# Two blocks of a hybrid model: half of the expert output kept in PSUM over all pairs, squares summed on GpSimd, attention order on TensorE written by hand

## The chip, the cores and the metric

One core of one Trainium2 chip runs the whole program in one launch. The metric is the device time of an execution in microseconds (us); 1607.19 us is the median of three runs of the kernel before (1606.79 to 1609.19). TensorE is called PE here, VectorE DVE, ScalarE ACT, GpSimd POOL and SyncE SP, as in the profile.

## The reference

The sequence has 512 tokens of width 1024, all in float32. The first block is a pre-norm block with six modulation vectors; its mixer is causal attention of 8 heads (with a forget gate) beside a pooling mixer, and its second half a gated feed-forward net with a short convolution:

```python
h = _rmsnorm(x, norm1_g[l]) * (1.0 + sc1) + sh1
z = h @ w_in[l]
attn = _fox_attention(q, k, v, log_f)
pool = _multiscale_pool(u, pool_w[l], pool_scale[l])
x = x + g1 * (concatenate([attn, pool]) @ w_out[l])
h = _rmsnorm(x, norm2_g[l]) * (1.0 + sc2) + sh2
x = x + g2 * _conv_ffn(h, ffn_up[l], ffn_conv_w[l], ffn_conv_b[l], ffn_down[l])
return _rmsnorm(x, final_g)
```

The second block has neighbourhood attention (8 heads, with an RMS norm of its output) beside a gated delta net, and a mixture of 64 experts of width 256, two to a token:

```python
x = x + concatenate([attn, dn], axis=-1) @ w_out
x = x + hierarchical_moe(rms_norm(x, ln2_g), ...)
hid = jax.nn.silu(xb @ w_gate[e]) * (xb @ w_up[e])
return hid @ w_down[e]
```

## The kernel before, in words

Activations lie transposed in SBUF, 128 features by 512 tokens a tile (xT, eight of them). A float32 product is made of three products of split operands, hi x hi, lo x hi and hi x lo (L171 to L173, the rows named pj); ACT makes the hi part (whi, hh: L164, L188) and DVE the lo part (wlo, hl: L165, L190 to L194). PSUM has eight banks, handed out by tags: mm, pa and pb two each, pc and gv one each (the function ps).

Most of the program is ordered by the framework's scheduler, which interleaves the instructions of independent parts on each engine. Two kinds of place are written in order by hand on PE: those inside a manual_schedule block, and before the change only the expert stage is one.

**Sums of squares.** An RMS norm over features is a sum over partitions. ColSums.add (L290) squares a tile on ACT (sq, L292) and multiplies it on PE by a 128x32 tile of ones (cs, L294), into one of four quarters of a bank. done (L297) copies the bank to SBUF on ACT (part, L299) and makes four small products with a weight column (cst, L302); rsqrt4 and row_bcast (rb, L321) follow. It is used for norm1 (col_sums), for norm2 (n2, eight squares, between the tiles of w_out), for the final norm and the second block's first norm together (csA and csB, eight squares each, between the tiles of the feed-forward's last third), and for the norm of the neighbourhood attention's output (cs, four squares).

**First attention.** head_pair(m) (L436) treats two heads. For each of four query tiles i it makes the logits of both heads (pS, L453, 64 rows of the array each), the softmax on DVE and ACT (L459 to L468), and the transposes of the probabilities (pT, L473) with their copies to SBUF (PT, L478 and L480). Then eight products with the values (po, L484). The scheduler sets projections of the next parts between these.

**Neighbourhood attention.** na_pairs has 32 units of a head and a tile: logits (nS, L772), softmax, and out (L783): two transposes (nT, L790), a copy on ACT, two products (npo, L794).

**Experts.** moe_round walks over 32 pairs of experts, expert pr_ with pr_ + 32. On PE, in this written order, are gate_up of a pair (pgu, L1568, 32 products), down of the pair before (pd, L1597, two halves n of eight products; the halves are scaled and split by ACT and DVE into og, hi and lo: L188 and L192), turn (phT, L1582, with the copies hT and OT), and combine of the pair before (L1604): for both halves n and four token tiles t, two products put the pair's rows back to their tokens (pcmb, L1610 and L1611) in one of four banks, and DVE adds the bank to the result xn (L1613). SP issues the weights' loads ahead of use (wgu at L1267, wd at L1277), each as soon as PE frees a buffer.

## Time and profile before

| | |
|---|---|
| median of three runs | 1607.19 us (1606.79 to 1609.19) |
| the profiled execution | 1610.31 us, span 1608.5 us |
| PE busy | 1519.7 us (94%), mean granted clock 0.973 |
| DVE / ACT / POOL busy | 893.3 / 507.8 / 208.7 us |
| chain that ended last | PE 78%, DVE 8%, DMA 5% of the span |
| DMA | 327.24 MB, 203 GB/s over the span |

The profile shows one execution. Its times are in microseconds from the first instruction. The granted clock is TensorE's clock as a share of full speed. A PE product's busy time overlaps that of the next one, since products are pipelined; the step from start to start is what one costs in a row of products. A float32 product that isn't split shows as two passes, so x2 in a row of the timeline is one product of cs, pS or po. What stands in brackets behind a row is the idle time ahead of it and what ended it.

### The profile page before, as it was taken

The page shows a single profiled execution, that of the slowest core. Times are in us where ns is not written, and L with a number is a line of the kernel's source. Part 1 is how long each engine was busy: PE and PEld are TensorE (multiplying, and loading weights), DVE is VectorE, ACT ScalarE, POOL GpSimd, SP SyncE. Part 2 cuts the span into 40 slices and gives each one's busy share as a digit, 9 for nine tenths or more (in the row PEclk, how much of TensorE's full clock was granted, in tenths as well). Part 3 has the DMA queues.
Part 4 walks back from the last instruction along what each step waited for, and adds up shares of the span by engine and source line. Part 5 has one row for each costly group of instructions (what it writes and reads, how often), then busy time and mean ns, then how long its engine had stood idle before and what let it go on. Part 6 is the DMA issues. An engine that isn't in the chain of part 4 may idle for free.

```text
span 1608.5 us, 20691 instructions
## 1 busy us (share of the span) xinstructions
PE 1519.7 (94%) x7541; PEld 1001.7 (62%) x7541; DVE 893.3 (56%) x1797; ACT 507.8 (32%) x937; POOL 208.7 (13%) x290
## 2 busy tenths in 40 slices
PE   6989999999999999998789999977999999999997
PEld 2756676788888886777667888864434434434443
DVE  3768666663564455256797666444445445445445
ACT  3553434442342344354334535410111111111111
POOL 0233000000000000223552330002100000000000
PEclk8979999999999999998989999988999999999999
DMA  8663132333223222354332133558899999999983
GB/s 310 224 208 113 66 132 77 119 99 99 92 98 99 92 81 77 101 165 112 89 104 75 36 88 95 213 237 314 320 406 419 418 415 419 417 413 417 409 364 107
DMA packets 81743, 327.24 MB, mean 203 GB/s; under 512 B 17624, under 2 KB 21336, under 8 KB 57312
## 3 DMA queue, kind: packets, MB, share of 16 engines
q1 hardware_dynamic: 80192, 320.58, 53.9%
q0 software_dynamic: 1440, 5.24, 0.9%
q8 instruction: 62, 1.02, 0.2%
q14 instruction: 49, 0.40, 0.1%
HBM read 317.32 MB, written 8.47 MB: 203 GB/s over the span
## 4 chain that ended last, share of the span: by engine, by line
PE 78%; DVE 8%; DMA 5%; issue 3%; POOL 3%; ACT 2%; SPq 0%; DVEq 0%; POOLq 0%; ACTq 0%
PE pgu L1568 13%; PE pj L171 10%; PE pj L172 10%; PE pj L173 10%; PE pd L1597 7%; PE pcmb L1610 5%; PE pcmb L1611 4%; DMA graw<-in_modw_dram 2%; PE cs L294 2%; PE pS L453 1%; DMA xg<-xs,tok_of 1%; DVE wlo L165 1%; DVE cv L828 1%; PE po L484 1%; PE npo L794 1%
## 5 line engine op out<-in xcount | busy, mean ns | idle before, releaser
L171 PE MATMUL pj<-hh,whi 128*128 128x512 f32 x640 | 258.5, 405 | 17.5 <-ACT cn L822 8.8
L173 PE MATMUL pj<-hh,wlo 128*128 128x512 f32 x640 | 256.2, 401 | 2.4 <-DVE wlo L165 2.4
L172 PE MATMUL pj<-hl,whi 128*128 128x512 f32 x640 | 256.5, 401 | 0.6 <-DVE hl L194 0.6
L1568 PE MATMUL pgu<-wgu,xw 128*64 128x512 f32 x1024 | 226.8, 595 | 0.0
L165 DVE TENSOR_TENSOR wlo<-wraw,whi 128x1024 fp32r<-128x1024 f32 (+4 forms) x126 | 153.1, 1217 | 67.3 <-ACT whi L164 64.1
L164 ACT ACTIVATE whi<-wraw 128x1024 fp32r<-128x1024 f32 (+4 forms) x126 | 129.2, 1028 | 150.5 <-PE pj L172 119.2
L1568 PEld LDWEIGHTS pgu<-wgu,xw 128*64 128x64 f32 x1024 | 70.7, 137 | 139.0 <-issue 138.9
L1613 DVE TENSOR_TENSOR xn<-xn,pcmb 128x512 f32<-128x512 f32 x256 | 155.7, 682 | 0.9 <-PE pcmb L1611 0.9
L171 PEld LDWEIGHTS pj<-hh,whi 128*128 128x128 f32 x640 | 122.7, 192 | 52.5 <-ACT cn L822 11.7
L173 PEld LDWEIGHTS pj<-hh,wlo 128*128 128x128 f32 x640 | 122.8, 192 | 34.3 <-issue 6.9
L172 PEld LDWEIGHTS pj<-hl,whi 128*128 128x128 f32 x640 | 122.8, 192 | 29.6 <-issue 4.4
L1572 ACT ACTIVATE sg<-pgu,agt 128x256 f32<-128x256 f32 x32 | 15.2, 476 | 335.3 <-PE pgu L1568 335.3
L1610 PE MATMUL pcmb<-og,OT 128*128 128x512 f32 x256 | 115.1, 450 | 1.4
L1597 PE MATMUL pd<-wd,hT 128*64 128x512 f32 x512 | 116.3, 596 | 0.0
L1574 DVE SCALAR_TENSOR_TENSOR hid<-pgu,agt,sg 128x256 f32<-128x256 f32 x32 | 15.5, 484 | 174.9 <-ACT sg L1572 174.9
L1611 PE MATMUL pcmb<-og,OT 128*128 128x512 f32 x256 | 101.7, 397 | 0.0
L192 DVE SCALAR_TENSOR_TENSOR og<-pd,agt,og 128x512 fp32r<-128x512 f32 x64 | 48.0, 751 | 77.3 <-ACT og L188 77.3
L1559 POOL COPY xw<-xgT 128x512 f32 x60 | 35.3, 617 | 409.6 <-PE pgu L1568 390.9
L1597 PEld LDWEIGHTS pd<-wd,hT 128*64 128x64 f32 x512 | 36.9, 138 | 73.3 <-issue 73.3
L1610 PEld LDWEIGHTS pcmb<-og,OT 128*128 128x128 f32 x256 | 48.0, 187 | 46.2 <-DVE xn L1613 27.0
L188 ACT ACTIVATE og<-pd,agt 128x512 fp32r<-128x512 f32 x64 | 44.1, 688 | 89.8 <-PE pd L1597 89.8
L172 PE MATMUL pj<-al,whi 128*128 128x512 f32 x176 | 69.8, 397 | 0.0
(430 smaller groups left out, 2499.0 us busy)
## 6 DMA issues: line engine op xcount, KB each, us to landing
wgu<-in_egu_dram SPq DMA_DIRECT2D x128, 1024.0 KB
wd<-in_ed_dram SPq DMA_DIRECT2D x62, 1024.0 KB
graw<-in_modw_dram SPq DMA_DIRECT2D x48, 512.0 KB
wraw<-in_wup_dram SPq DMA_DIRECT2D x42, 512.0 KB
wraw<-in_win_dram SPq DMA_DIRECT2D x38, 512.0 KB
wraw<-in_wdn_dram SPq DMA_DIRECT2D x20, 512.0 KB
wraw<-in_wout_dram SPq DMA_DIRECT2D x16, 512.0 KB
E<-gscr SPq DMA_DIRECT2D x16, 256.0 KB
```

The lines of the kernel that those rows point to most:

```text
L164: nc.scalar.activation(hi, raw, AF.Copy)
L165: nc.vector.tensor_tensor(lo, raw, hi.bitcast(F32), op=ALU.subtract)
L171: nc.tensor.matmul(p, whi, hh, start=first, stop=False)
L172: nc.tensor.matmul(p, whi, hl, start=False, stop=False)
L173: nc.tensor.matmul(p, wlo, hh, start=False, stop=last)
L188: nc.scalar.activation(hi, src, AF.Identity, scale=scale, bias=0.0 if bias is None else bias)
L192: nc.vector.scalar_tensor_tensor(lo, src, scale, hi.bitcast(F32), op0=ALU.mult, op1=ALU.subtract)
L1568: nc.tensor.matmul(gu[64 * i:64 * i + 64, :], xw[:, j, 64 * i:64 * i + 64], wts.gu[e][j], start=(j == 0), stop=(j == 7))
L1597: nc.tensor.matmul(pd[64 * i:64 * i + 64, :], hT[:, j, 64 * i:64 * i + 64], wts.d[e][:, j, n * 512:n * 512 + 512], start=(j == 0), stop=(j ...
L1610: nc.tensor.matmul(pc, OT[:, ts], a, start=True, stop=False)
L1611: nc.tensor.matmul(pc, OT[:, ts], b, start=False, stop=True)
L1613: nc.vector.tensor_tensor(v, v, pc, op=ALU.add)
```

## The change

- ColSums keeps its sum in SBUF: the first square goes straight to an accumulator, each further one is added to it on POOL; done makes the four cst products from it with a column of ones. csN takes a slot named cv for cs; the others take a tile of a new pool of two buffers, sums. norm1 keeps the old way (ColSumsPE).
- head_pair is a written order on PE: logits(i + 1) ahead of turn(i), all eight value products together at the end. na_pairs too: out takes two units, transposes of both, then their products, alternating.
- combine keeps half n = 0 in four banks (mm, gv, mm, pc) from the first pair to the last and adds it to xn once, at the last pair; half n = 1 goes through the two banks of pb and is added to xn at each pair. The written order goes from half to half. phT moves from pb to pa, and pxg (the gather of tokens) from mm to pb.

```diff
--- before.py
+++ after.py
...
     rst = ctx.enter_context(ExitStack())
     rp = rst.enter_context(tc.tile_pool(name="resid", bufs=1, side="right"))
+    ast = ctx.enter_context(ExitStack())
+    accp = ast.enter_context(tc.tile_pool(name="sums", bufs=2, side="right"))
+    def acc():
+        return accp.tile([128, S], F32, tag="acc", name="acc")
     xT = [rp.tile([128, S], F32, name=f"xT{j}") for j in range(8)]
     nc.sync.dma_start(vec, A["vecs"])
...
     class ColSums:
 
+        def __init__(self, acc, tag):
+            self.a, self.tag, self.first = acc, tag, True
+        def add(self, s, scale=1.0):
+            if self.first:
+                nc.scalar.activation(self.a, s, AF.Square, scale=scale)
+                self.first = False
+                return
+            sq = sp_.tile([128, S], F32, tag="tmp", name="sq", bufs=4)
+            nc.scalar.activation(sq, s, AF.Square, scale=scale)
+            nc.gpsimd.tensor_tensor(self.a, self.a, sq, op=ALU.add)
+        def done(self):
+            pt = ps(self.tag, "cst")
+            for t in range(4):
+                nc.tensor.matmul(pt[:, t:t + 1], self.a[:, t * 128:t * 128 + 128], ones32[:, 0:1], start=True, stop=True)
+            return pt[:, 0:4]
+    class ColSumsPE:
+
         def __init__(self, n, tag):
             self.p, self.n, self.tag, self.j = ps(tag, "cs"), n, tag, 0
...
             return pt[:, 0:4]
     def col_sums(srcs, tag="pc"):
-        cs = ColSums(len(srcs), tag)
+        cs = ColSumsPE(len(srcs), tag)
         for s in srcs:
             cs.add(s)
         return cs.done()
...
                 nc.vector.tensor_tensor(Bd[e], B[e].rearrange("p (a b) -> p a b", a=4),
                                         C("cmask").unsqueeze(1).to_broadcast([128, 4, 128]), op=ALU.add)
                 PT.append([ap.tile([128, S - 128 * b], F32, tag=f"PT{b}", name=f"PT{b}", bufs=2) for b in range(4)])
-            for i in range(4):
+            def logits(i):
                 n = (i + 1) * 128
                 P = []
                 for e in range(2):
...
                     rcp = sp_.tile([128, 1], F32, tag="rcp", name="rcp")
                     nc.vector.reciprocal(rcp, mx[:, 3:4])
                     nc.vector.tensor_scalar(p_[:, 0:n], p_[:, 0:n], rcp, None, op0=ALU.mult)
+                return P
+            def turn(i, P):
                 for e in range(2):
                     p_ = P[e][1]
                     pt = ps("pb", "pT")
...
                             nc.scalar.activation(dst, src, AF.Copy)
                         else:
                             nc.vector.tensor_copy(dst, src)
-            for b in range(4):
-                for e in range(2):
-                    hd = 2 * m + e
-                    nc.tensor.matmul(po[64 * e:64 * e + 64, b * 128:S], Vn[:, b, hd * 64:hd * 64 + 64],
-                                     PT[e][b], start=(b == 0), stop=(b == 3))
+            with tc.manual_schedule(engines={mybir.EngineType.PE}):
+                P = logits(0)
+                for i in range(1, 4):
+                    P, before = logits(i), P
+                    turn(i - 1, before)
+                turn(3, P)
+                for b in range(4):
+                    for e in range(2):
+                        hd = 2 * m + e
+                        nc.tensor.matmul(po[64 * e:64 * e + 64, b * 128:S], Vn[:, b, hd * 64:hd * 64 + 64],
+                                         PT[e][b], start=(b == 0), stop=(b == 3))
             new_mix(m)
             split_h(mh[m], ml[m], po)
...
-        n2 = ColSums(8, "pb")
+        n2 = ColSums(acc(), "pb")
         gemv_done(3, acc3)
         w_out(0)
         gemv_done(4, acc4)
...
                 al.append(fp.tile([128, S], F32R, tag="al", name="al", bufs=11))
                 split_h(ah[-1], al[-1], act)
             if third == 2:
-                csA, csB = ColSums(8, "pc"), ColSums(8, "gv")
+                csA, csB = ColSums(acc(), "pc"), ColSums(acc(), "gv")
...
+    ast.close()
...
             nc.vector.reciprocal(r, mx[:, 3:4])
             nc.vector.tensor_scalar(P[u], P[u], r, None, op0=ALU.mult)
-        def out(u):
-            m, e, b = u
-            h = 2 * m + e
-            if (b, e) == (0, 0):
-                po[m] = ps("pc", "npo")
-            pt = ps("pa", "nT")
+        def out(us):
+            T = {}
+            for u in us:
+                m, e, b = u
+                if (b, e) == (0, 0):
+                    po[m] = ps("pc", "npo")
+                pt = ps("pa", "nT")
+                for i in range(2):
+                    nc.tensor.transpose(pt[:, i * 128:i * 128 + 128], P[u][:, i * 128:i * 128 + 128], ident)
+                T[u] = slot("nPT", "nPT", 2, (128, 256))
+                nc.scalar.activation(T[u], pt[:, 0:256], AF.Copy)
             for i in range(2):
-                nc.tensor.transpose(pt[:, i * 128:i * 128 + 128], P[u][:, i * 128:i * 128 + 128], ident)
-            T = slot("nPT", "nPT", 2, (128, 256))
-            nc.scalar.activation(T, pt[:, 0:256], AF.Copy)
-            for i in range(2):
-                nc.tensor.matmul(po[m][64 * e:64 * e + 64, b * 128:b * 128 + 128],
-                                 vsh[b + i][:, h * 64:h * 64 + 64], T[:, i * 128:i * 128 + 128],
-                                 start=(i == 0), stop=(i == 1))
-            if (e, b) == (1, 3):
+                for u in us:
+                    m, e, b = u
+                    h = 2 * m + e
+                    nc.tensor.matmul(po[m][64 * e:64 * e + 64, b * 128:b * 128 + 128],
+                                     vsh[b + i][:, h * 64:h * 64 + 64], T[u][:, i * 128:i * 128 + 128],
+                                     start=(i == 0), stop=(i == 1))
+            if b == 3:
                 nc.scalar.activation(perm(at[m]), unperm(po[m]), AF.Copy)
                 if done:
                     done(m)
-        for i in range(0, len(units), 2):
-            logits(units[i])
-            logits(units[i + 1])
-            if i:
-                out(units[i - 2])
-                out(units[i - 1])
-        out(units[-2])
-        out(units[-1])
+        with tc.manual_schedule(engines={mybir.EngineType.PE}):
+            for i in range(0, len(units), 2):
+                logits(units[i])
+                logits(units[i + 1])
+                if i:
+                    out(units[i - 2:i])
+            out(units[-2:])
 
     dcw = cp.tile([128, 60], F32, name="dcw")
...
-    cs = ColSums(4, "gv")
+    cs = ColSums(slot("cv", "csN", 6), "gv")
     scan_prep(3)
     po1 = scan_pair(1)
     cs.add(at[0])
...
         nc.gpsimd.indirect_dma_start(out=xg, out_offset=None, in_=xs,
                                      in_offset=bass.IndirectOffsetOnAxis(ap=tok, axis=0))
         for q in range(2):
-            p = ps("mm", "pxg")
+            p = ps("pb", "pxg")
             for j in range(4):
                 nc.tensor.transpose(p[:, j * 128:j * 128 + 128], xg[:, (4 * q + j) * 128:(4 * q + j) * 128 + 128], ident)
             nc.vector.tensor_tensor(dst[:, 4 * q:4 * q + 4, :], p.rearrange("p (j s) -> p j s", j=4),
...
         def turn(pr_, hid):
-            pt = ps("pb", "phT")
+            pt = ps("pa", "phT")
...
                 split_h(*ab[n], pd, scale=gt[:, 1, pr_:pr_ + 1])
             return ab
-        def combine(OT, ab, final=False):
-
-            for n, (a, b) in enumerate(ab):
-                for t in range(4):
-                    pc = ps(("mm", "gv", "mm", "pc")[t], "pcmb")
-                    ts = slice(t * 128, t * 128 + 128)
-                    nc.tensor.matmul(pc, OT[:, ts], a, start=True, stop=False)
-                    nc.tensor.matmul(pc, OT[:, ts], b, start=False, stop=True)
+        kept = []
+        def combine(OT, ab, start=False, stop=False):
+            if start:
+                kept.extend(ps(("mm", "gv", "mm", "pc")[t], "pkept") for t in range(4))
+            for n, t in ((0, 0), (0, 1), (1, 0), (0, 2), (1, 1), (0, 3), (1, 2), (1, 3)):
+                a, b = ab[n]
+                ts = slice(t * 128, t * 128 + 128)
+                pc = ps("pb", "pcmb") if n else kept[t]
+                nc.tensor.matmul(pc, OT[:, ts], a, start=(n == 1 or start), stop=False, skip_group_check=(n == 0))
+                nc.tensor.matmul(pc, OT[:, ts], b, start=False, stop=(n == 1 or stop), skip_group_check=(n == 0))
+                if n or stop:
                     v = xn[t][:, n * 512:n * 512 + 512]
                     nc.vector.tensor_tensor(v, v, pc, op=ALU.add)
-                    if final:
+                    if stop:
                         nc.sync.dma_start(out[ts, n * 512:n * 512 + 512], v)
 
...
                     ab = down(*prev[:2])
                 cur = turn(pr_, hid)
                 if prev is not None:
-                    combine(prev[2], ab)
+                    combine(prev[2], ab, start=(pr_ == 1))
                 prev = (pr_,) + cur
-            combine(prev[2], down(*prev[:2]), final=True)
+            combine(prev[2], down(*prev[:2]), stop=True)
     moe_round("a", wts, gt_a, first)
     nc.vector.tensor_reduce(cmax, cnt, axis=AX.X, op=ALU.max)
```

**PE at the end of csA and csB**, where the projections of the second block (pj) stand on both sides. A row is line, operation, destination and operands, then the columns, and what it waits for (the engine's name stands before _49). Before:

```order
L171 MATMUL pj_4956<-hh,whi 128x512
L294 MATMUL cs<-sq,ones_65 32x512 [waits Activation_49]
L172 MATMUL pj_4956<-hl,whi 128x512
L173 MATMUL pj_4956<-hh,wlo 128x512
L171 MATMUL pj_4957<-hh,whi 128x512
L172 MATMUL pj_4957<-hl,whi 128x512
L173 MATMUL pj_4957<-hh,wlo 128x512
L171 MATMUL pj_4956<-hh,whi 128x512
L172 MATMUL pj_4956<-hl,whi 128x512
L173 MATMUL pj_4956<-hh,wlo 128x512
L302 MATMUL cst<-w_66,part 128x1 [waits Activation_49]
L302 MATMUL cst<-w_66,part 128x1 x3
```

The last of the sixteen cs stands here, ahead of the first cst by eight projections. Now:

```order
L177 MATMUL pj_4961<-hh,whi 128x512
L178 MATMUL pj_4961<-hl,whi 128x512
L179 MATMUL pj_4961<-hh,wlo 128x512
L177 MATMUL pj_4960<-hh,whi 128x512
L309 MATMUL cst<-ones_65,acc 128x1 [waits Pool_49]
L309 MATMUL cst<-ones_65,acc 128x1 x3
L178 MATMUL pj_4960<-hl,whi 128x512
L179 MATMUL pj_4960<-hh,wlo 128x512
L177 MATMUL pj_4961<-hh,whi 128x512
L309 MATMUL cst<-ones_65,acc 128x1 [waits PE_49,Pool_49]
L309 MATMUL cst<-ones_65,acc 128x1 x3
L178 MATMUL pj_4961<-hl,whi 128x512
```

No cs is left, cst waits for POOL in place of ACT, and from the first product of the next projection (pj_4956 before, pj_4960 now) to the first cst there are 13 projections where 21 were.

**PE at the end of head pair 3**, with the projections of the feed-forward around it. Before:

```order
L172 MATMUL pj_1743<-hl,whi 128x512
L173 MATMUL pj_1743<-hh,wlo 128x512
L484 MATMUL po<-PT_1531,Vn 64x512 [waits DVE_49]
L473 MATMUL pT<-cst,P 128x128 [waits DVE_49,Activation_49]
L473 MATMUL pT<-cst,P 128x128 x3
L171 MATMUL pj_1744<-hh,whi 128x512
L172 MATMUL pj_1744<-hl,whi 128x512
L173 MATMUL pj_1744<-hh,wlo 128x512
L484 MATMUL po<-PT_1539,Vn 64x512 [waits DVE_49]
L484 MATMUL po<-PT_1532,Vn 64x384 [waits Activation_49]
L484 MATMUL po<-PT_1540,Vn 64x384 [waits Activation_49]
```

One value product (po) stood ahead of the last four transposes, with three projections in between, and the others behind them. Now:

```order
L505 MATMUL pT<-cst,P 128x128 [waits DVE_49,Activation_49]
L505 MATMUL pT<-cst,P 128x128 x3
L505 MATMUL pT<-cst,P 128x128 [waits DVE_49]
L505 MATMUL pT<-cst,P 128x128 x3
L523 MATMUL po<-PT_1543,Vn 64x512 [waits DVE_49]
L523 MATMUL po<-PT_1551,Vn 64x512 [waits DVE_49]
L523 MATMUL po<-PT_1544,Vn 64x384 [waits Activation_49]
L523 MATMUL po<-PT_1552,Vn 64x384 [waits Activation_49]
```

All eight value products (the last four are cut off here) stand behind the last transposes, with nothing between.

**PE in the combine of a pair**, pkept the kept banks, pcmb the others, numbers of buffers included. The last tile of half 0 and half 1 before:

```order
L1610 MATMUL pcmb_10475<-og_10445,OT_10364 128x512
L1611 MATMUL pcmb_10475<-og_10445,OT_10364 128x512
L1610 MATMUL pcmb_10479<-og_10453,OT_10364 128x512 [waits DVE_49,Activation_49]
L1611 MATMUL pcmb_10479<-og_10453,OT_10364 128x512
L1610 MATMUL pcmb_10483<-og_10453,OT_10364 128x512 [waits DVE_49]
L1611 MATMUL pcmb_10483<-og_10453,OT_10364 128x512
L1610 MATMUL pcmb_10487<-og_10453,OT_10364 128x512 [waits DVE_49]
L1611 MATMUL pcmb_10487<-og_10453,OT_10364 128x512
L1610 MATMUL pcmb_10491<-og_10453,OT_10364 128x512 [waits DVE_49]
```

Each tile of half 1 waited for DVE, whose adds to xn free the banks. Now, the same part from the second tile on:

```order
L1659 MATMUL pkept_9506<-og_10381,OT_10308 128x512
L1660 MATMUL pkept_9506<-og_10381,OT_10308 128x512
L1659 MATMUL pcmb_10403<-og_10389,OT_10308 128x512 [waits Activation_49]
L1660 MATMUL pcmb_10403<-og_10389,OT_10308 128x512 [waits DVE_49]
L1659 MATMUL pkept_9507<-og_10381,OT_10308 128x512
L1660 MATMUL pkept_9507<-og_10381,OT_10308 128x512
L1659 MATMUL pcmb_10409<-og_10389,OT_10308 128x512 [waits PE_49]
L1660 MATMUL pcmb_10409<-og_10389,OT_10308 128x512
L1659 MATMUL pkept_9508<-og_10381,OT_10308 128x512
L1660 MATMUL pkept_9508<-og_10381,OT_10308 128x512
L1659 MATMUL pcmb_10415<-og_10389,OT_10308 128x512 [waits DVE_49]
L1660 MATMUL pcmb_10415<-og_10389,OT_10308 128x512
```

The first tile of half 1 (pcmb_10403) moved from the fifth place to the third, and its two products wait for the og of that half, hi by ACT and lo by DVE; of DVE's adds only the last two tiles wait, the first of which stands here (pcmb_10415).

## Rows read from the trace of the kernel before

**Rows 1.** The page, part 1: engine busy us (share of the span) xinstructions.

```profile
PE 1519.7 (94%) x7541; PEld 1001.7 (62%) x7541; DVE 893.3 (56%) x1797; ACT 507.8 (32%) x937; POOL 208.7 (13%) x290
```

**Rows 2.** Windows: us, busy PE, PEld, DVE, ACT, POOL; PEclk, DMA share, GB/s.

```profile
120.00:200.00 80.00, 77.85 (x386) 49.06 (x384) 62.57 (x213) 33.10 (x91) 14.63 (x15) 1.00 0.28 92
200.00:240.00 40.00, 40.00 (x180) 30.01 (x180) 25.18 (x42) 13.86 (x19) 0.56 (x5) 1.00 0.40 132
...
500.00:620.00 120.00, 120.00 (x519) 95.96 (x517) 60.95 (x74) 41.75 (x55) 0.00 (x0) 1.00 0.27 88
...
1160.00:1560.00 400.00, 398.88 (x1743) 162.59 (x1739) 189.41 (x318) 56.94 (x107) 31.25 (x54) 1.00 1.01 414
```

**Rows 3.** Timeline, PE ahead of a cs product: start us, us, engine, line.

```profile
257.21 0.39 PE L173 MATMUL pj<-hh,wlo 128*128 128x512 f32 x1
257.44 0.39 PE L171 MATMUL pj<-hh,whi 128*128 128x512 f32 x1
257.75 1.05 PE L294 MATMUL cs<-sq,ones 128*32 128x512 f32 x2
```

**Rows 4.** Timeline, PE: two and four cs products together.

```profile
244.96 1.30 PE L294 MATMUL cs<-sq,ones 128*32 128x512 f32 x4
...
608.70 2.91 PE L294 MATMUL cs<-sq,ones 128*32 128x512 f32 x8
```

**Rows 5.** One line's instructions, L823 on POOL: duration ns min/median/max.

```profile
L823 POOL TENSOR_TENSOR cn<-cn,RR x12: 1279/1437/2075, 705.5 to 847.9; 128x512 f32<-128x512 f32 x12
```

**Rows 6.** Timeline at the end of csA/csB: DVE, ACT, PE.

```profile
642.46 1.46 DVE L604 SCALAR_TENSOR_TENSOR xT<-pj,modT,xT 128x512 f32<-128x512 f32 x2
...
643.94 0.61 ACT L292 ACTIVATE sq<-xT 128x512 f32<-128x512 f32 x1
...
652.91 0.95 PE L302 MATMUL cst<-w,part 128*128 128x1 f32 x8
...
657.65 0.65 PE L321 MATMUL rb<-cst,rr 128*128 128x128 f32 x4 [0.96 <-DVE rr L629]
```

**Rows 7.** By shape, DVE, 200 to 280, then 690 to 720: us, ns.

```profile
L165 DVE TENSOR_TENSOR wlo<-wraw,whi 128x1024 fp32r<-128x1024 f32 x8 | 9.8, 1222 | 5.5 <-ACT whi L164 5.4
...
L165 DVE TENSOR_TENSOR wlo<-wraw,whi 128x1024 fp32r<-128x1024 f32 x7 | 9.5, 1364 | 2.7 <-DMA vscr<-vn 2.1 <-ACT whi L164 0.6
```

**Rows 8.** Timeline, PE: logit products of head pairs 0 and 1.

```profile
120.78 0.48 PE L453 MATMUL pS<-kT,zq 64*128 64x128 f32 x2
...
141.81 0.49 PE L453 MATMUL pS<-kT,zq 64*128 64x128 f32 x4
```

**Rows 9.** Windows of the value products (L484) alone, PE and PEld.

```profile
118.00:133.00 15.00, 3.87 (x16) 1.06 (x16) 0.96 0.37 123
...
141.00:150.00 9.00, 2.82 (x16) 1.60 (x16) 1.00 0.32 94
```

**Rows 10.** The chain of waits in the expert stage: start us, us, what.

```profile
1288.79 7.02 PE pgu L1568 x32
...
1303.95 7.02 PE pgu L1568 x32
```

**Rows 11.** Timeline of a combine: DVE, PE's weight load and PE.

```profile
1300.03 0.75 DVE L192 SCALAR_TENSOR_TENSOR og<-pd,agt,og 128x512 fp32r<-128x512 f32 x1 [0.99 <-ACT og L188]
...
1300.70 3.67 DVE L1613 TENSOR_TENSOR xn<-xn,pcmb 128x512 f32<-128x512 f32 x6
...
1302.63 0.19 PEld L1610 LDWEIGHTS pcmb<-og,OT 128*128 128x128 f32 x1 [0.30 <-DVE xn L1613]
...
1303.88 0.65 PE L1568 MATMUL pgu<-wgu,xw 128*64 128x512 f32 x2
```

**Rows 12.** Windows, the stretch behind the wait at 95.4.

```profile
99.40:119.30 19.90, 19.17 (x41) 9.69 (x41) 12.07 (x52) 10.23 (x24) 7.29 (x6) 0.50 0.50 169
```

**Rows 13.** Timeline, PE: the wait itself, with what ended it.

```profile
99.44 1.22 PE L453 MATMUL pS<-kT,zq 64*128 64x256 f32 x2 [4.03 <-DVE mx L461]
```

**Rows 14.** Windows, the end of the expert stage.

```profile
1560.00:1600.00 40.00, 39.83 (x171) 16.85 (x170) 22.05 (x37) 5.63 (x10) 0.00 (x0) 1.00 0.30 110
```

## Prediction

> **What bounds the kernel now.** I read the page first, for what is busy, then the windows, for where, and then the timelines of the places that the change touches. The page shows TensorE (PE) busy for 1519.7 us of a span of 1608.5 us, 94% [rows 1]. The windows say where that holds: PE is busy 40.00 of 40 us at 200 to 240, 120.00 of 120 at 500 to 620, 77.85 of 80 at 120 to 200, and 398.88 of 400 in the expert stage [rows 2]. [...] So in these stretches a PE instruction that goes away shortens the program by its own length, and work that moves from PE to an idle engine is free until PE has to wait for it. POOL (GpSimd) is 0.56 us busy in the 40 us of the first of them, and not at all in the second.
>
> **The squares.** Before, each ColSums.add gives PE one 32x512 product that the trace shows as two passes (x2). One that stands alone runs 1.05 us, and while it runs, PE does nothing else; the projections ahead of it stand 0.23 us apart [rows 3]. I take its length as its price. Two together take 1.30 us and four together 2.91 [rows 4]. The change removes 28 of them: 8 of n2 (two pairs and four alone, 2 x 1.2 + 4 x 1.05 = 6.6 us), 16 of csA and csB (two fours and eight alone, 2 x 2.91 + 8 x 1.05 = 14.2), 4 of cs (alone, 4.2). That is 25 us of PE at 98 to 100% load. The four ACT copies named part go too, off PE. Nothing is added to PE: the four cst products read the accumulator in place of part.
>
> What comes instead is a chain on POOL, 22 adds of 128x512 one after the other. The trace has adds or products of two 128x512 tiles on POOL at another line: 1.28 us at least, 1.44 in the median, 2.08 at most [rows 5]; I take 1.4, since most of the adds meet an idle POOL and a chain of one kind. Some 31 us of POOL's time, hidden wherever PE has projections to go on with. It is not hidden at the end, where cst must wait for the last add.
>
> For csA/csB the last two xT are made by 1.46 us of DVE from 642.46, their squares start at 643.94, and before, PE came to the first cst at 652.91 and to rb at 657.65 [rows 6]. The new chain has four adds behind those squares: from about 644.6 four times 1.4 ends near 650.2 if the second accumulator waits for the last one, and its first accumulator is ready 1.4 earlier, near 648.8. The PE order puts the first cst eight projections sooner, 1.9 us, and the four cs behind 644 are gone, 4.2 us, so PE comes to it near 646.8 on the old time scale and stands there some 2 us, and under 1 us at the second. Then cst, the small POOL and DVE steps and rb follow as before. PE has 10.1 us less up to 644 (the two fours and four of those alone, 5.8 + 4.3); behind that rb comes some 3.4 us after the second cst, as before, near 654 against 657.65, of which I count 3 us. I take 13, with ends 10 (adds of 2.08 us, 2.7 us more wait) and 14.2. For n2 the same sum is 6.6 less a wait of about 1.2 that remains (POOL ends one add behind the last square, and the part copy no longer stands between): 5.5, ends 3 and 6.6. For cs the PE order puts cst some 40 short products sooner, directly where POOL has one add left: 4.2 less about 1.7, 2.5, ends 1 and 4.2.
>
> [...]
>
> POOL's adds also run beside DVE. The same DVE split takes 1222 ns in a stretch with POOL idle and 1364 in one where POOL works [rows 7]. DVE has 25 of 40 us to do at 200 to 240 [rows 2], so 12% on the instructions that meet an add does not reach PE in the middle; at the ends it makes the chain longer and stands in the ends above.
>
> **The attention order.** A logit product of one head (64 rows) that has its partner of the other head directly beside it costs nothing more: two of 128 columns take 0.49 us together, and one alone takes 0.48 [rows 8]. So an adjacency is worth one product, 0.42 to 1.05 us by columns (estimated from those rows, as the columns). The order shows 6 of 16 pairs adjacent before, 9 after: about 2 us. The value products of a head pair take 2.82 us where all stand together and 3.87 where they are broken [rows 9]; three of the four pairs are broken, the last two a little less than the first, so that grouping is worth at most 3 us. Against it, these products now stand right behind the last transposes, so that PE waits for the copies in between. I take 3 in all (ends 0 and 5). The neighbourhood attention gains at most half a microsecond: its grouped products are 128 wide and cost the same by fours.
>
> **The expert stage.** In the chain of waits a pair takes 15.16 us from pgu to pgu [rows 10], and it goes through PE alone. In the combine PE stands on DVE: lo1, the second og of DVE, ends at 1300.78, DVE's adds follow (six in 3.67 us), and PE's last products wait 0.30 us each on them; the next pgu starts at 1303.88 [rows 11]. After, only four adds are on DVE and PE waits for two of them, long done. But the third tile in the written order is now the first of half 1, and its second matmul needs lo1, so PE stands from about 1300.4 to 1300.85; eleven products in steps of 0.23 follow [rows 3], the last at about 1303.2, and pgu 0.3 behind: 1303.6 against 1303.88. I take 0.25 us for each of 30 pairs: 7.5 us. Ends: 0, if the kept banks bring a wait of their own, and 0.75, all waits of the combine, 22 us. At the last pair the eight adds come all at the end, as before.
>
> **The sum.** 13 + 5.5 + 2.5 + 3 + 7.5 = 31.5 us. Against the profiled execution (1610.31 us, with 1.8 us around its span) that makes 1578.8; this execution stood 3.1 us over the median of the runs, 1607.19, from which I take it: 1607.2 - 31.5 = 1575.7 us.
>
> **Rivals.**
>
> *The POOL chain is late and the clock falls.* [...] If adds of 2.08 us make the three waits longer by 5 us together, and each is followed by a stretch of 7 us at half clock (3.5 us lost), the sum loses 15.5: 1591. For it: PE has nothing else between cst and the add, and DVE's 142 ns more beside a busy POOL [rows 7]. [...] Chance 0.17.
>
> *DMA is the bound of the expert stage.* The loads run at 414 GB/s with a DMA share of 1.01 at 1160 to 1560 [rows 2]. If that is the ceiling, PE gains only until the lead of the loads is used up. For it: the share. Against: the DMA share is only 0.30 at 1560 to 1600 [rows 14], so the last weights land over 20 us before PE ends, and 7.5 us of gain do not use that up. Without the expert gain: 1607.2 - 24 = 1583. Chance 0.08.
>
> *All waits of the combine go.* If lo1 is no wait, the expert stage gives 0.6 to 0.75 us a pair, some 12 us more: 1560 to 1564. Against it: lo1 is tied to the end of pd, which doesn't move. Chance 0.1.
>
> *The written attention order stalls PE.* PE takes its instructions in order, and a written order lets it stand in front of a transpose whose softmax isn't ready, where the scheduler would have let it do a projection. The row at 99.44 is such a wait: 4.03 us on DVE's mx, and 10 us more lost at half clock behind it [rows 12, 13], 14 us in all. It decides from three such places on (a head pair has one, at its last transposes): 3 x 14 = 42, more than the 31.5, and the time is 1607.2 + 10.5 = 1618. For it: nothing but that row. Against: the order still shows projections between the pieces of each head pair, and PE is busy 77.85 of 80 us there. Chance 0.05.
>
> *The order does nothing.* Only the relative order of the attention is fixed, projections still stand inside it, and 7 of 16 pairs stay broken: the time is 1579, inside the forecast's range. Chance 0.1. The forecast has the other 0.5.
>
> **How the numbers follow.** The forecast's own range is 1568 to 1583. For 8 in 10 it must take in the late POOL chain, 1591, and half of the case where all waits of the combine go, 1562: 1562 to 1592. A change of 0.2% (3.2 us) is about what a measurement of this kernel tells from none. Faster: all cases but the stalls in attention and a part of the late chain with worse prices, 0.92; within: 0.03; slower: 0.05.
>
> **What would show it.** The cs products are gone from PE outside the first norm, and acc stands on POOL 22 times, 1.3 to 1.6 us each. PE waits for POOL before cst in three places, 1 to 3 us each, and the granted clock behind stays at 1.00. The step from pgu to pgu falls from 15.16 to about 14.9 us, with PE waiting on DVE's og at the third place of the combine, and on xn nowhere. The DMA share stays near 1.00. It would be wrong if a stretch of 0.50 stands behind a cst, if a pair takes 15.1 us or more, or if PE's busy share at 120 to 200 falls.

## The result and the profile after

The changed kernel takes 1585.71 us (median of four runs, 1583.53 to 1587.61) against 1606.99 us of the kernel before on the same chip: the ratio is 0.9865, with a 95% interval of 0.9848 to 0.9883. That is 21 us faster, in the forecast's range (1562 to 1592) and 10 us short of its likeliest value, 1575.7. The profiled execution took 1585.05 us, span 1583.3, against 1610.31 and 1608.5 before.

Two rows of the page of the changed kernel, the engines' busy time (part 1) and the new adds (part 5: busy us, mean ns of one | idle before, releaser):

```profile
PE 1484.3 (94%) x7485; PEld 1006.7 (64%) x7485; DVE 843.9 (53%) x1673; ACT 503.3 (32%) x933; POOL 247.0 (16%) x314
...
L304 POOL TENSOR_TENSOR acc<-acc,sq 128x512 f32<-128x512 f32 x21 | 33.7, 1623 | 392.8 <-ACT sq L303 392.6
```

PE is still 94% busy, with 35 us less to do than before [rows 1]. An add on GpSimd takes 1.62 us in the mean where I had taken 1.4 [rows 5]. These are 21 adds, seven each of n2, csA and csB; with the three of the neighbourhood attention's norm (csN) there are 24, where the prediction and the expectation of e4 write 22.

The stages by their first and last rows in the timelines, in us of the two profiled executions:

| stretch | before | after | gain | forecast |
|---|---|---|---|---|
| start to first logits of attention | 87.6 | 90.6 | -3.0 | 0 |
| first logits to last value product | 112.2 | 103.7 | 8.5 | 3 |
| from there to rb of n2 | 64.9 | 62.7 | 2.1 | 5.5 |
| from there to rb of csA/csB | 393.0 | 382.6 | 10.5 | 13 |
| from there to the last npo | 351.0 | 351.4 | -0.4 | 0 |
| from there to the routing (prank) | 70.5 | 68.3 | 2.2 | 2.5 |
| from there to the first combine | 53.4 | 52.8 | 0.6 | 0 |
| first to last combine | 467.6 | 463.3 | 4.3 | 7.5 |
| from there to the end | 8.5 | 7.9 | 0.6 | 0 |

The gains make 25.3 us between these two executions, of which the one before stood 3.3 us above its median. The first two lines also hold stretches at a lower granted clock (in the changed kernel 30 to 40 us at 0.64 in the mean and 102.1 to 115.6 at 0.50; before [rows 12]), which differ from run to run: the first logits stand at 86.7 us in e8 and at 92.0 in e3, with the same order. So these two lines can each be off by some us. And the attention order alone moves 1.4 us from the second line to the third: from the last value product to rb of n2 are 66.3 us in e3, which has that order and the old sums, against 64.9 before.

At the end of n2 (timeline, GpSimd and PE):

```profile
248.72 3.40 POOL L304 TENSOR_TENSOR acc<-acc,sq 128x512 f32<-128x512 f32 x2 [8.13 <-ACT sq L303]
...
252.17 1.87 PE L309 MATMUL cst<-ones,acc 128*128 128x1 f32 x8 [2.32 <-POOL acc L304]
```

PE stands 2.32 us at cst for the last two adds, 1.70 us each. The window behind it has PE busy without a break, at a granted clock of 0.50:

```profile
252.20:259.00 6.80, 6.80 (x22) 5.82 (x23) 1.44 (x4) 0.02 (x1) 1.02 (x1) 0.50 0.03 11
```

At the end of csA/csB (timeline: GpSimd, DVE, DVE, PE):

```profile
618.18 6.68 POOL L304 TENSOR_TENSOR acc<-acc,sq 128x512 f32<-128x512 f32 x4 [2.81 <-ACT sq L303]
...
620.43 3.30 DVE L198 SCALAR_TENSOR_TENSOR hl<-xT,gs,hh 128x512 fp32r<-128x512 f32 x2 [1.33 <-ACT hh L194]
...
623.66 1.89 DVE L677 TENSOR_SCALAR xT<-xT,vec 128x512 f32<-128x512 f32 x2
...
627.49 0.60 PE L177 MATMUL pj<-hh,whi 128*128 128x512 f32 x1 [3.29 <-DVE xT L643]
```

Here PE stands 3.29 us, and not for an add: it waits for DVE's xT. DVE is late because its two hl took 3.30 us and the two scalings of xT 1.89 us, beside four adds of GpSimd. Before, two hl took 1.41 us. This wait is not in the prediction. Behind it the clock falls as it did behind n2 (windows):

```profile
627.60:631.10 3.50, 3.50 (x9) 2.75 (x10) 1.53 (x2) 3.43 (x6) 2.90 (x2) 0.51 0.69 175
```

In the combine (the chain of waits: start us, us, what):

```profile
1262.04 0.70 ACT og L194
1262.73 0.03 issue
1262.76 0.76 DVE og L198
1263.52 0.04 issue
1263.56 0.50 PE pcmb L1660
...
1266.51 7.02 PE pgu L1612 x32
...
1281.51 0.57 PE pgu L1612
```

From pgu to pgu are 15.00 us, where it was 15.16 [rows 10]. The chain leaves PE now: it goes through the og of ACT and DVE to the second product of the third tile, as the prediction said. Then the last tile waits as well (timeline, PE's weight load):

```profile
1265.78 0.19 PEld L1659 LDWEIGHTS pcmb<-og,OT 128*128 128x128 f32 x1 [0.28 <-DVE xn L1663]
```

### The profile page after: what moved, and what is told of

Read it like the earlier page. It is cut to its first block, busy times and chain, and to the rows that moved or that the text cites. A ratio compares the mean times of both kernels' runs of the same rounds, so it can differ in the third digit from the quotient of the medians.

```text
span 1583.3 us, 20312 instructions
## 1 busy us (share of the span) xinstructions
PE 1484.3 (94%) x7485; PEld 1006.7 (64%) x7485; DVE 843.9 (53%) x1673; ACT 503.3 (32%) x933; POOL 247.0 (16%) x314
## 4 chain that ended last, share of the span: by engine, by line
PE 71%; DVE 11%; DMA 6%; ACT 4%; POOL 3%; issue 3%; SPq 1%; POOLq 0%; ACTq 0%; DVEq 0%
PE pgu L1612 13%; PE pj L177 10%; PE pj L179 10%; PE pj L178 10%; PE pd L1641 7%; PE pcmb L1660 2%; DVE wlo L171 2%; DMA graw<-in_modw_dram 2%; PE pcmb L1659 2%; DVE og L198 2%; DMA xg<-xs,tok_of 1%; ACT og L194 1%; DVE cv L872 1%; PE pS L482 1%; PE pkept L1659 1%
## 5 line engine op out<-in xcount | busy, mean ns | idle before, releaser
L1663 DVE TENSOR_TENSOR xn<-xn,pcmb 128x512 f32<-128x512 f32 x128 | 85.1, 685 | 33.7 <-PE pcmb L1660 33.7
L304 POOL TENSOR_TENSOR acc<-acc,sq 128x512 f32<-128x512 f32 x21 | 33.7, 1623 | 392.8 <-ACT sq L303 392.6
L179 PE MATMUL pj<-ah,wlo 128*128 128x512 f32 x176 | 69.3, 394 | 0.0
L177 PE MATMUL pj<-ah,whi 128*128 128x512 f32 x176 | 69.3, 394 | 0.0
```

Source lines behind the costliest of these rows:

```text
L177: nc.tensor.matmul(p, whi, hh, start=first, stop=False)
L179: nc.tensor.matmul(p, wlo, hh, start=False, stop=last)
L1663: nc.vector.tensor_tensor(v, v, pc, op=ALU.add)
```

## The experiments

Ten kernels follow. Ratios are to the kernel before, timed beside each of them; e5 has one execution alone, and no ratio. Times of stages are from one profiled execution of each kernel.

**Which part gives what.** Each of the three parts of the change alone, on the kernel before. First the experts, the lines of the diff in pxg, phT, combine and its two calls:

> The kernel before with the expert part of the change alone (half of the output kept in four banks). Theory A (the second product of the third tile waits for DVE's og of half 1, and the last tile for DVE's add): a pair goes from 15.16 to 15.00 us as in the changed kernel, some 5 us in all, about 1602 us. Rival B (my forecast, 0.25 us a pair): 7.5 us, about 1599.5. Rival C (the loads are the bound): no gain, 1607.

Measured: 0.9981 (0.9960 to 1.0002), 1605.85 us, some 3 us less, which the interval alone does not tell from nothing. The chain does:

```profile
1254.31 7.02 PE pgu L1568 x32
...
1269.31 7.02 PE pgu L1568 x32
```

15.00 us a pair, theory A, and the first to the last combine take 463.2 us, as in the changed kernel. B's time is just outside the interval (0.9952 against 0.9960), and C is out, since the pair got shorter.

The sums, the lines of the diff in ColSums, the pool sums, and the four places that make one:

> The kernel before with the sums of squares on GpSimd alone. Theory A (the adds on GpSimd slow VectorE beside them and end late, and TensorE's waits there bring stretches at the lower clock): about 15 us gained (2 at n2, 10.5 at csA/csB, 2.5 at cs), 1592 us, with the waits of 2.3 and 3.3 us in the profile. Rival B (my forecast): 21 us, 1586.

Measured: 0.9895 (0.9865 to 0.9924), 1589.53 us, 17 us gained. That lies between A and B, and the interval holds both. In its profile the 2.32 us of n2 and the 3.29 us of csA/csB stand as in the changed kernel:

```profile
250.76 1.05 PE L309 MATMUL cst<-ones,acc 128*128 128x1 f32 x8 [2.32 <-POOL acc L304]
```

But in this execution the clock stayed at 1.00 behind n2's wait, and the stretch from the last value product to rb of n2 took 59.2 us, 5.7 less than before, about the 5.5 that I had forecast for n2. In the changed kernel it took 62.7. Behind the 3.29 us of csA/csB the clock did fall, to 0.50 for 6.8 us.

The attention order, the lines in head_pair and na_pairs:

> The kernel before with the written attention order alone. Theory A (the order itself gives the 8.5 us that the stretch from the first logits to the last value product got shorter): 1598 to 1600 us. Rival B (my forecast of 3 us; the rest was a shorter stretch at the lower clock by chance): about 1604, and the stretch from the first logits to the last value product 109 us long.

Measured: 0.9967 (0.9949 to 0.9985), 5.3 us by the ratio, 1603.0 us. That is between A and B. Windows of the logits alone, before and in this kernel, and of the value products alone, before and in this kernel (PE's and PEld's busy us; PEclk, DMA share, GB/s):

```profile
86.00:200.00 114.00, 26.34 (x64) 9.53 (x64) 0.91 0.37 121
```

```profile
86.00:200.00 114.00, 21.79 (x64) 8.05 (x64) 0.94 0.40 133
```

```profile
86.00:200.00 114.00, 13.53 (x64) 5.77 (x64) 0.91 0.37 121
```

```profile
86.00:200.00 114.00, 10.87 (x64) 6.10 (x64) 0.94 0.40 133
```

The logits cost 4.6 us less and the value products 2.7. Some of it is clock, which was 0.94 against 0.91. The stretch from the first logits to the last value product was 104.3 us, not B's 109. But the 8.5 us of theory A are in part chance: this stretch takes 106.3 to 112.2 us in the four profiles with the old order (before, e1, e2, e9; mean 109.4) and 101.0 to 108.1 in the eight with the new one (mean 104.0). The means differ by 5.3 us, of which the next stretch takes back 1.4 (66.3 us in e3): 3.9 us, inside the interval of the ratio.

The three ratios multiply to 0.9844, some 25 us. The whole change has 0.9865 (0.9848 to 0.9883). The product lies just under that interval, but each of its factors has an interval of its own, so the parts add up as far as these runs tell.

**What is lost at the sums.** The same change with all its 24 adds on VectorE:

```diff
-            nc.gpsimd.tensor_tensor(self.a, self.a, sq, op=ALU.add)
+            nc.vector.tensor_tensor(self.a, self.a, sq, op=ALU.add)
```

> The changed kernel with the 22 adds on VectorE in place of GpSimd. Theory A (the loss at n2 and csA/csB comes from GpSimd's slow adds and what they do to VectorE): an add takes 0.7 us, the 128x512 instructions of VectorE beside it are back at their own length (0.48 and 0.75 us), the waits of 2.3 us before cst of n2 and 3.3 us ahead of the last projections of csA/csB shrink to under 1 us, no stretch at the lower clock follows, 1578 to 1582 us. Rival B (VectorE is the late engine there anyhow, and more work on it makes it later): as long or longer than the changed kernel, 1585 to 1590.

Measured: 0.9787 (0.9760 to 0.9813), 1573.15 us: 12 us better than the changed kernel, more than A had said. The groups of DVE at 560 to 660 in three kernels (busy us, mean ns of one), before, changed, and with the adds on VectorE:

```profile
L192 DVE SCALAR_TENSOR_TENSOR hl<-xT,gs,hh 128x512 fp32r<-128x512 f32 x8 | 5.7, 749 | 6.6 <-ACT hh L188 6.6
L637 DVE TENSOR_SCALAR xT<-xT,vec 128x512 f32<-128x512 f32 x8 | 3.6, 481 | 0.0
```

```profile
L198 DVE SCALAR_TENSOR_TENSOR hl<-xT,gs,hh 128x512 fp32r<-128x512 f32 x8 | 10.1, 1306 | 4.7 <-ACT hh L194 4.7
L677 DVE TENSOR_SCALAR xT<-xT,vec 128x512 f32<-128x512 f32 x8 | 6.9, 894 | 0.0
```

```profile
L304 DVE TENSOR_TENSOR acc<-acc,sq 128x512 f32<-128x512 f32 x14 | 8.8, 685 | 0.4 <-ACT sq L303 0.4
...
L198 DVE SCALAR_TENSOR_TENSOR hl<-xT,gs,hh 128x512 fp32r<-128x512 f32 x8 | 5.6, 748 | 0.0
...
L677 DVE TENSOR_SCALAR xT<-xT,vec 128x512 f32<-128x512 f32 x8 | 3.7, 478 | 0.0
```

With GpSimd beside it, the same hl takes 1306 ns in place of 749, the same scaling 894 in place of 481. With the adds on VectorE an add takes 685 ns, and both are back at their own length. PE's wait at csA/csB shrinks to

```profile
614.31 0.47 PE L177 MATMUL pj<-hh,whi 128*128 128x512 f32 x1 [0.24 <-DVE xT L643]
```

and from n2's rb to that of csA/csB it is 377.0 us, 16 less than before and 5.6 less than in the changed kernel. The stretch of n2 takes 59.3 us (62.7 in the changed kernel), and no stretch at 0.50 stands behind either place. These two and 1.1 us at cs make 10.1 us of the 12; the rest is not traced to a place, and this profiled execution is the fastest of e4's six. In e8, which has the same sums, the three places give 3.3, 4.5 and 1.0 us.

Then a kernel that puts only the last two adds of n2, csA and csB on VectorE:

```diff
+            self.j += 1
-            nc.gpsimd.tensor_tensor(self.a, self.a, sq, op=ALU.add)
+            (nc.vector if self.j > 5 else nc.gpsimd).tensor_tensor(self.a, self.a, sq, op=ALU.add)
```

> The changed kernel with only the last two adds of n2, csA and csB on VectorE, all others on GpSimd. Theory A (at csA/csB the loss is VectorE slowed by GpSimd's adds of the tiles before; at n2 it is the slow last adds): the wait before cst of n2 falls under 1.5 us, the wait of 3.3 us ahead of the last projections of csA/csB stays, as the adds of tiles 4 and 5 are still on GpSimd; 3 to 5 us better than the changed kernel. Rival B (the loss is the length of the chain behind the last squares alone): the wait of 3.3 us goes as well, and the time is that with all adds on VectorE, 12 us better.

Measured: 0.9827 (0.9801 to 0.9853), 1581.36 us, 6 us better than the changed kernel by the ratios, where A had said 3 to 5 and B 12. In the timeline of PE the cst of n2 has no wait, and at csA/csB there is the same wait as before the edit:

```profile
250.44 1.05 PE L310 MATMUL cst<-ones,acc 128*128 128x1 f32 x8
...
621.52 0.47 PE L177 MATMUL pj<-hh,whi 128*128 128x512 f32 x1 [3.29 <-DVE xT L644]
```

So the two losses have two causes: at n2 the slow adds ahead of cst, at csA/csB DVE. At 621 PE waits for DVE's xT and not for an add. What the wait at n2 costs can now be read: the stretch takes 59.4 us here without it, 60.5 in e6 with it and the clock at 1.00 behind it, 62.7 in the changed kernel with the clock at 0.50 behind it. So some 1.1 us are the wait and 2.2 the clock.

To have the second by itself, a kernel got adds on GpSimd that nobody reads. First the kernel before:

```diff
             nc.tensor.matmul(self.p[32 * q:32 * q + 32, :], ones32, sq, start=(j < 4), stop=(j >= self.n - 4))
+            if self.a is not None:
+                nc.gpsimd.tensor_tensor(self.a, self.a if self.j else sq, sq, op=ALU.add)
```

> The kernel before, sums of squares still on TensorE, and beside them the sixteen adds of csA and csB once more on GpSimd, into tiles that nobody reads. Theory A (GpSimd's adds slow VectorE, and VectorE holds up TensorE at the last projections of csA/csB): the hl there go from 0.75 to about 1.3 us and TensorE waits some 2 to 3.5 us on VectorE's xT before the first projection behind 643, though nobody waits for an add; 3 to 6 us slower than the kernel before. Rival B (the wait came from the chain of adds ahead of cst): VectorE's instructions as long as before, no such wait, the same time within 2 us.

Measured: 1.0001 (0.9978 to 1.0024), no wait. The time is B's, but neither theory holds: VectorE is as slow as A says, and PE does not wait for it:

```profile
L194 DVE SCALAR_TENSOR_TENSOR hl<-xT,gs,hh 128x512 fp32r<-128x512 f32 x8 | 11.3, 1454 | 6.6 <-ACT hh L190 6.6
L642 DVE TENSOR_SCALAR xT<-xT,vec 128x512 f32<-128x512 f32 x8 | 7.7, 987 | 0.0
```

From one pair of xT tiles to the next PE takes 11.4 to 13.1 us here with the cs, as before, and DVE still waits in each such step, for ACT or PE, up to 2.17 us at a time. In the changed kernel the cs are gone: the first step, beside two adds, takes 8.4 us, and the next two, beside four adds each, 9.8 and 10.0, set by DVE with its slow instructions and its wait of 1.3 to 1.7 us for ACT's hh. So the loss should need both, the slow instructions and the shorter step. That was tested on the kernel with the sums on VectorE, where the step is 8.4 us:

```diff
             nc.vector.tensor_tensor(self.a, self.a, sq, op=ALU.add)
+            if self.more:
+                nc.gpsimd.tensor_tensor(sq, sq, sq, op=ALU.add)
```

> The kernel with the sums on VectorE (e4), and beside them an add on GpSimd of each square of csA and csB with itself, which nobody reads. Theory A' (after the probe on the kernel before: GpSimd slows VectorE always, but that reaches TensorE only where the products of the squares are gone and VectorE is the tighter engine): the hl of csA/csB go from 0.75 to over 1.1 us, the step between two pairs of xT tiles grows from 8.4 us by 2 to 4 us, TensorE waits on VectorE's xT again, and the kernel is 4 to 9 us slower than e4, ratio to the kernel before 0.981 to 0.985. Rival B' (only the adds that someone waits for cost time): the ratio of e4, 0.979, and no wait.

Measured: 0.9824 (0.9806 to 0.9842), against 0.9787 of e4. The groups of DVE and PE's wait:

```profile
L198 DVE SCALAR_TENSOR_TENSOR hl<-xT,gs,hh 128x512 fp32r<-128x512 f32 x8 | 11.9, 1524 | 0.0
...
L679 DVE TENSOR_SCALAR xT<-xT,vec 128x512 f32<-128x512 f32 x8 | 8.5, 1085 | 0.0
```

```profile
628.87 0.77 PE L177 MATMUL pj<-hh,whi 128*128 128x512 f32 x1 [5.78 <-DVE xT L645]
```

The hl doubled, PE stands 5.78 us on DVE, and nothing in the trace waits for these adds (ACT's squares of the last two pairs wait for DVE's xT too). The intervals of e10 and e4 overlap a little (0.9806 to 0.9813), so the ratios alone would be thin; the stretch from n2's rb to that of csA/csB is 385.2 us against 377.0. A' holds.

**What is lost at the combine.** Only the order of tiles:

```diff
-            for n, t in ((0, 0), (0, 1), (1, 0), (0, 2), (1, 1), (0, 3), (1, 2), (1, 3)):
+            for n, t in ((0, 0), (0, 1), (0, 2), (1, 0), (0, 3), (1, 1), (1, 2), (1, 3)):
```

> The changed kernel with the first tile of half 1 one place later in the combine, (0,0) (0,1) (0,2) (1,0) (0,3) (1,1) (1,2) (1,3). Theory A (two waits stand in each pair, on og of half 1 and, for want of a third bank for half 1, on the adds; whichever is avoided, the other grows): the wait of 0.49 us on DVE's og goes, the last tile waits 0.4 to 0.7 us on DVE's xn, and a pair still takes 15.0 us. Rival B (the wait on og alone is the loss): 14.7 us a pair, 9 us less in all.

Measured once: 1587.95 us, 0.3 us above the slowest run of the changed kernel. The chain:

```profile
1250.55 0.70 DVE xn L1663
...
1252.03 7.02 PE pgu L1612 x32
...
1265.69 0.70 DVE xn L1663
...
1267.17 3.15 PE pgu L1612 x13
```

15.14 us a pair, and 467.6 us from the first to the last combine, as before the change. The wait on og is gone, and 0.70 us of DVE's xn stands in the chain in its place, a little worse than A's 15.0. B is out.

Then the same order with a third bank for half 1:

```diff
-                pc = ps("pb", "pcmb") if n else kept[t]
+                pc = ps(("pb", "pb", "pa", "pb")[t], "pcmb") if n else kept[t]
```

> The same order with a third bank for half 1: the tile (1,2) goes to the tag pa. Theory A: no wait is left in the combine and a pair takes 14.6 to 14.7 us, 10 us less than the changed kernel, with the loads at some 430 GB/s. Rival C (the loads are the bound below 15 us): a pair stays near 14.9 to 15.0 us on the average, PE waits for wgu or wd, or the waits come after some pairs, and the time falls by 0 to 4 us.

Measured: 0.9754 (0.9730 to 0.9778), 1568.2 us, 18 us below the changed kernel, more than A's 10: a pair takes 14.56 us, 0.44 less than in the changed kernel, and the first to the last combine 448.6 us in place of 463.3, 14.7 less. Another 2.2 us stand at n2, where the clock did not fall in this execution. The chain, the windows, and whom SP's loads wait for:

```profile
1257.85 7.02 PE pgu L1612 x32
...
1272.41 7.02 PE pgu L1612 x32
```

```profile
1160.00:1260.00 100.00, 100.00 (x456) 44.52 (x454) 34.65 (x56) 14.87 (x28) 8.24 (x14) 1.00 1.01 421
```

```profile
SPq L1321 <- DMA wgu<-in_egu_dram: 30.7, 18, 2.1
SPq L1311 <- DMA wd<-in_ed_dram: 26.6, 17, 2.1
```

PE is busy 100.00 of 100 us. The loads run at 421 GB/s, where 14.56 us a pair would need 432 (an estimate: six loads of 1024 KB a pair), and SP now waits for loads to land, where in the changed kernel its loads waited for PE alone. No window of this stage that was read goes above 421 in the changed kernel, e6 or e8. So the loads are at the highest rate that these runs show, as rival C says, but the lead lasts to the end: the pairs keep 14.56 us from the third to the last, and PE waits for no weights.

**Both together**, the adds on VectorE and the third bank:

> The changed kernel with all adds on VectorE and the combine with three banks for half 1. Theory A (the two gains are independent): 12 us and 10 us less than the changed kernel, ratio to the kernel before about 0.972. Rival C (the loads become the bound as the expert stage gets shorter): 12 to 16 us less, 0.976 to 0.979.

Measured: 0.9694 (0.9671 to 0.9717), 1558.49 us. This is 27 us faster than the changed kernel, and 49 us than the one before. That is better than both theories had said. The two gains add up: from the ratios of e4, e6 and the changed kernel follows 0.9787 x 0.9754 / 0.9865 = 0.9677, inside the interval.

## Why the prediction was right and wrong

The time lies in the stated range and outside the forecast's own, 1568 to 1583: the stated range takes in the late POOL chain, and something of that kind came. Of the five terms cs came out as written, attention gave more than forecast, n2, csA/csB and the experts gave less, and the sum of 31.5 us came out as 21. So the time is in the range by the range's width, and not by its terms.

- **What bounds** was right: PE in the stretches that were read, so that products that go give time by their length. The 25 us of cs are gone from PE (24.96 us busy in the trace before). Where PE hardly waits (0.24 us, in e4 and e8) the stretch of csA/csB takes 377.0 and 378.1 us, against 390.8 to 393.0 in the four profiles with the cs: 13 to 16 us, about the 14.2 of the products themselves.
- **n2**: 5.5 forecast, 2.1 in the table. With the 1.4 us that the attention order moves into this line, the squares gave 3.5 us here; against e3 they gave 5.7 in e6, where the same wait stood and the clock stayed up, and 6.9 in e4, e7 and e8, where no wait stood. e2 gave 5.7 as well, against the kernel before. So "6.6 less a wait of about 1.2" was near in time (6.8, with the 1.30 us of [rows 4] where the sum has 1.2): PE stands 2.32 us, twice what was worked out, but the stretch gets only 1.1 us longer by it. What the sum put at nothing is the clock, which fell to 0.50 for 6.8 us behind the wait in the changed kernel's profile and cost 2.2 us. The rival that the clock falls behind a wait, at 0.17, happened here. It took 7 us at half clock behind each of three waits, a length that was my estimate and that no row gives; this profile has 6.8 us at 0.50 behind n2, 3.5 us at 0.51 behind the wait at csA/csB, and 1.00 behind cst of the third (980 to 1000 us).
- **csA/csB**: the sum of 13 came out as 10.5. The step that failed is "12% on the instructions that meet an add does not reach PE in the middle". The DVE instructions there take 74 and 86% more, not 12%. I had read the 12% from a mean, and the single instructions of that row, wlo at 690 to 720 before the change, say something else (duration ns min/median/max):

```profile
L165 DVE TENSOR_TENSOR wlo<-wraw,whi x7: 1204/1220/2254, 691.7 to 718.8; 128x1024 fp32r<-128x1024 f32 x7
```

Six of the seven ran at their own length, 1204 to 1226 ns, and the one that lay beside GpSimd's products took 2254, 85% more. So the size was in the trace before, hidden by a mean over instructions most of which met no add. And DVE had 25 of 40 us of work at n2, but at csA/csB the removal of the cs itself took its slack away. The loss there is the 3.29 us of PE's wait and the 3.4 us at 0.50 behind it. The wait at cst that I had priced at 2 us was 0.5, but that is no success: PE had stood for 3.29 us just ahead of it.
- **cs**: 2.5 forecast, 2.2 measured; 2.0 to 2.2 in e2, e5 and e6, and 0.7 in e7, where a stretch of 3.4 us at 0.50 falls into it.
- **Attention**: 3 forecast, 5.3 (2.4 to 8.2) measured by e3; the logits took 4.6 us less, more than the 2 us that I had counted by adjacency, and a part of that is clock. The slower rival, a written order that stalls PE, did not come: the wait at the first logits was there before and after (4.03 and 4.51 us), and no other of the order's new waits is longer than 0.91 us.
- **Experts**: the mechanism was right, the size off. "0.25 us for each of 30 pairs" was 0.16: the og wait as forecast (0.49 us), but the last tile waits 0.28 us more on DVE's add, where I had written "long done". The rival with all waits gone needed a third bank (e6); moving the order alone turned one wait into the other (e5).
- **DMA as the bound**: not in the changed kernel, where SP's loads waited for PE. In e6 they run at 421 GB/s and wait for loads to land, and the lead covers it, as was argued.
- **The signs** that were to show the forecast wrong: a stretch of 0.50 does stand behind a cst, at n2; a pair takes 15.00 us, less than 15.1; PE's busy time at 120 to 200 fell a little, 76.64 of 80 us where it was 77.85, though the attention got shorter. Of the waits before cst that were to be 1 to 3 us in three places only that of n2 is (2.32; the others are 0.50 and 0.71).
- **GpSimd's adds**: I took 1.4 us for one; the trace has 1.62 in the mean, so the rows that I took it from were low. Beside these adds VectorE's hl, which reads two SBUF tiles, takes nearly twice as long (1306 ns against 749), the scaling, which reads one tile, is slowed as well (894 against 481), and with the adds on VectorE the kernel was 12 us faster. The runs show the lengths; by what path GpSimd's adds slow VectorE was not shown.

## What to carry to other kernels

Work that was moved to an idle engine had a price on its neighbour here (VectorE's hl took 1306 ns beside GpSimd's adds and 749 without them). For another kernel, read what the neighbour's single instructions cost beside that engine, by their longest and not by a mean over many that met no such work, and read the neighbour's slack after the change, not before: here the change itself took slack away, since PE's step from one pair of xT tiles to the next got shorter (11.4 to 13.1 us before, 8.4 to 10.0 after). Where an accumulator takes banks from a rotation, count the banks that are left against the adds that must free them; with two left, both written orders that were tried here kept a wait (15.00 and 15.14 us a pair), and a third bank took it away (14.56).

## What the runs showed of the hardware

- The 21 adds of 128x512 on GpSimd in the changed kernel took 1.27 us at the least and 1.62 us in the mean, 2.07 at most; the same add on VectorE (e4) took 0.685 in the mean.
- Beside such adds (changed, e9, e10), VectorE's hl of 128x512, which reads SBUF alone, took 1.3 to 1.5 us in the mean in place of 0.75, and the scaling of xT 0.9 to 1.1 in place of 0.48, whether anyone waited for the adds or not.
- Not every VectorE instruction paid. In the first attention of the changed kernel the scaling P<-P,rcp of 128x128, from SBUF to SBUF, took 0.70 to 1.31 us in the four cases that lay almost wholly beside a 128x512 instruction of GpSimd, and 0.27 to 0.28 in the others; P<-pS,Bd,mx of the same size, which reads PSUM, took 0.33 to 0.35 us either way.
- The same wait of 2.32 us of PE before the cst of n2 is in four profiles (changed, e2, e5, e6). In the changed kernel and in e5 a stretch of 6.8 us at a granted clock of 0.50 follows, in e2 and e6 it stays at 1.00. The price of the same short wait is therefore not the same from run to run: the stretch took 62.7 and 62.8 us with the clock down, 59.2 and 60.5 with it up.
- Behind the wait of 3.29 us at csA/csB (changed, e2, e5, e6, e7) and that of 5.78 (e10) 3.4 to 6.8 us at 0.50 follow in every profile; where the wait is 0.24 us (e4, e8) or none (before, e1, e3, e9) the clock there stays at 1.00.
- The loads of the expert stage ran at 420 to 421 GB/s in e6 while SP waited for earlier loads to land, though PE's step would have taken 432 (the estimate above); in the changed kernel, where SP waited for PE alone, they ran at 418 to 421 between 1160 and 1520 us.
